# One transformer layer on one core: an opening in another order (rows ahead of weights, modulation in two column halves), and the first attention units prepared in twelve steps

## The chip, the cores and the metric

The kernel runs on one core of one Trainium2 chip. The metric is device time in microseconds (us) of one execution. All timed runs below are of the same program on the same inputs; the profile is one further execution that the hardware profiler recorded.

## What is computed

One layer of a hybrid diffusion backbone, over 2048 latent tokens of width 1024 and 256 context tokens, all in f32. Cut to what bears on this case:

```python
mod_x = silu(c) @ w_mod + b_mod          # w_mod (1024, 6*1024); six vectors of 1024
sh1, sc1, g1, sh2, sc2, g2 = split(mod_x, 6)
mod_c = silu(c_ctx) @ w_mod + b_mod
sh1c, sc1c = the first two of split(mod_c, 6)

h_c = rmsnorm(ctx, norm1_g) * (1 + sc1c) + sh1c
p_c = h_c @ w_in[:, :256]                # keys and values of the context only
h_x = rmsnorm(x, norm1_g) * (1 + sc1) + sh1
p_x = h_x @ w_in                         # k 128 | v 128 | q 512 | u 512 | vg 512 | gate 1024 | gate 1024
k, q = rmsnorm per head, rotary on latent tokens
attn = softmax(q @ [k_c; k_x].T) @ [v_c; v_x]      # 8 query heads, 2 key heads, head width 64
gm = gelu(u) * (gm_ws @ rmsnorm(gelu(vg)) + gm_bs) # in chunks of 128 tokens
x = x + g1 * ((sigmoid(ga) * (attn @ w_br_attn) + sigmoid(gb) * (gm @ w_br_gm)) @ w_out)
h2 = rmsnorm(x, norm2_g) * (1 + sc2) + sh2
x = x + g2 * (square(relu(h2 @ w_ff1)) @ w_ff2)
```

So nothing of a projection can begin before the vectors `sh1`, `sc1`, `sh1c` and `sc1c` are known: 1024 x 2048 of `w_mod` have to be read and multiplied with two conditions first.

## The kernel before, in words

The program is written out straight, with no loops on the chip, in four stages: `project()` (normalization, modulation, the input projection, keys, queries, the gated branch), `attend()` (32 units: four blocks of 512 queries, four pairs of heads in each, two of them to a key head), `merge()` and `ffn()`. `build()` (from L1464) calls them in turn.

A precise product is made of three matmuls: each operand is split into a rounded high part and a remainder, and `mm3` (L176) issues high x high, high x low and low x high; these are the lines L178, L179 and L180 in every view. `split` (L143) makes the two parts: the cast of the high part is L146 (ACT) or L148 (DVE), and the remainder is L150. `transposes` (L182, the matmul is L184) turns tiles on TensorE (PE) with an identity.

**The opening.** `mod_head` (L239) loads the two conditions, `norm1_g` and the first 2048 of `b_mod` in columns (one value of 4 bytes to a partition at a time, L244 to L253), on the queues of SP and ACT. It makes silu, a column per k (k counts eight slices of 128 channels) and condition, and multiplies for each k four halves of 512 columns of `w_mod` with a stationary operand two columns wide (L270): four banks, 32 matmuls. The rows of the result are copied (L276), turned by 16 small transposes, and `b_mod` is added (L285); L289 makes the scale `G1 = (1 + sc1) * norm1_g`, and `S1` holds the shift. Both are one tile of 8 k x 2 conditions. The rows of ctx are loaded at k = 2, those of x at k = 6, behind the weights of the k before them on SP's queue.

`h_build` (L434) is a generator with a step for each k: the rows of normalized x are turned on PE, ACT applies scale and shift (L443), DVE casts (L148) and subtracts (L150). `project()` (L706) takes all eight steps for the context, then all eight for block 0, and then the products of the keys and values: `token_mm` (L479) sums eight k for two tiles of 128 tokens into one bank, 256 columns each. The first two weight tiles of `w_in` (`w_tiles`, L451: four k of 256 columns each) serve these. After them come the wide products of 512 columns: queries, the two halves of the gated branch, and the gates.

**The gates and what lies among them.** For each block of 512 tokens, `project()` runs 16 gate steps (c = 0 to 3, two destinations, m = 0 and 1); `gate_mm` is 24 products of 512 columns. Behind each step of blocks 1 to 3 one step of `mod_rest` (L291) runs: the other four modulation vectors, summed on DVE one k a step, each with a load of 512 KB of `w_mod`. Behind the steps of the last block with c > 1, or c = 1 and the second destination, seven steps of `tail()` (L1470) run: it prepares units 0 and 1 of attention. A unit loads its queries from DRAM (`load`), ACT casts them (`cast`), DVE subtracts (`remainder`), and PE turns high parts and remainders, ACT copying the result (`queries`, the copy is L1567). `maxima` takes two banks, multiplies turned queries with keys (L1589), and DVE reduces each bank to its maxima (L1595 for the context, L1600 else); `reference` makes of them the offset of the softmax, and `low_queries` turns the remainders with it. `kb_build` (L757) makes copies of the keys with halves of partitions exchanged. When all gates are done `build()` runs out what is left of `tail()` and of `mod_rest`, and `attend()` begins with the scores of unit 0 (L1633).

**What sets the order.** A scheduler places the instructions of each engine as dependences and buffers allow. `order()` (L1504) adds rules after the program is written: new tiles of one tag (buffer class) are taken in program order; instructions in a range of `pins` keep program order on all engines, those in `fixed` on PE and DVE, those in `steady` on all but SP. Only `pins` around the loads of gm_ws and rope and around `mod_rest` lie in `project()`; `fixed` covers `attend()`. There are eight PSUM banks of 512 columns.

## Time and profile before

| what | value |
|---|---|
| time, median of 3 runs | 3026.22 us (3025.89 to 3028.58) |
| the profiled execution's own time | 3029.68 us |
| its span | 3027.9 us |
| PE busy | 2989.3 us, 99% |
| DVE busy | 2028.3 us, 67% |
| ACT busy | 1354.3 us, 45% |
| POOL (GpSimd) busy | 563.2 us, 19% |
| DMA, mean | 160 GB/s |
| mean granted clock of PE | 0.998 |
| span from 0 to 71 us: PE busy | 58.20 us |
| span from 71 to 711 us: PE busy | 640.00 us |
| span from 711 to 773 us: PE busy | 59.07 us |

The span is what the profiler saw between the first and the last instruction; the execution's own time is 1.8 us more. PE's busy time is the union of its matmuls, which overlap. It tells that PE worked on something, not at what width: a matmul with two columns of result rows and one with 128 count alike. In the views a row reads line, engine, operation, output and inputs by tile name without buffer numbers; a square bracket holds the idle time ahead of the row and who ended it. Tile names begin with the tag: `w` for weights, `t` for the working buffers, `m` for rows of x and ctx, `ts` for small vectors, `b` for PSUM banks.

### The profile page before, as it was taken

To read this page: it belongs to the slowest core of one execution; us is meant where nothing else is said; L and a number is where in the kernel's file an instruction comes from. 1 tells how busy PE (TensorE), PEld (TensorE's weight loads), DVE (VectorE), ACT (ScalarE), POOL (GpSimd) and SP (SyncE) were. 2 spreads that over 40 slices of the span, in tenths; PEclk is the share of its full clock that TensorE was granted. 3 is DMA by queue.
4 is the path that set the end of the run, shared out by engine and by line. 5 is a ranking of instruction groups with operands and counts; after the bars stand their busy time and mean duration, and the time that the engine had idled before them with its cause. 6 is when DMAs were issued, how large, how long until landed. Compare 5 with 4: busy or idle time off the path is not lost.

```text
span 3027.9 us, 39850 instructions
## 1 busy us (share of the span) xinstructions
PE 2989.3 (99%) x14980; PEld 2304.8 (76%) x14980; DVE 2028.3 (67%) x2984; ACT 1354.3 (45%) x2043; POOL 563.2 (19%) x419
## 2 busy tenths in 40 slices
PE   8999999999999999999999999999999999999999
PEld 4888888887665656655888878887878888888887
DVE  5837567586777778886655688776665666654455
ACT  4443434343555555554322254444553344444432
POOL 0000000000689999990000000000000000000000
PEclk9999999999999999999999999999999999999999
DMA  6354656645000000012755549889766544436665
GB/s 217 109 184 119 220 155 187 183 129 164 29 15 12 15 22 19 26 33 95 240 180 180 167 141 329 310 304 316 241 210 222 197 154 151 152 144 218 210 221 194
DMA packets 332179, 485.53 MB, mean 160 GB/s; under 512 B 33969, under 2 KB 166321, under 8 KB 331986
## 3 DMA queue, kind: packets, MB, share of 16 engines
q1 hardware_dynamic: 324002, 478.38, 47.9%
q10 hardware_dynamic: 7984, 4.61, 0.5%
q8 instruction: 117, 1.92, 0.3%
q14 instruction: 76, 0.62, 0.1%
HBM read 348.56 MB, written 134.35 MB: 159 GB/s over the span
## 4 chain that ended last, share of the span: by engine, by line
PE 93%; DVE 3%; DMA 2%; ACT 1%; issue 1%; SPq 1%; ACTq 0%; DVEq 0%
PE b L1244 13%; PE b L1245 13%; PE b L1243 13%; PE b L178 11%; PE b L180 11%; PE b L179 11%; PE b L1633 9%; PE b L1653 8%; PE b L1589 2%; PE b L184 2%; DVE ts L1600 1%; DMA ts<-in_b_mod 1%; PE b L1695 0%; DMA w<-in_w_in 0%; DMA f<-x_d 0%
## 5 line engine op out<-in xcount | busy, mean ns | idle before, releaser
L1349 DVE TENSOR_TENSOR f<-f,f 128x1024 fp32r<-128x1024 f32 x224 | 264.5, 1221 | 251.4 <-ACT f L1348 251.3
L1600 DVE TENSOR_REDUCE ts<-b 128x1 f32<-128x512 f32 x512 | 311.7, 682 | 98.4 <-PE b L1589 98.3
L1244 PE MATMUL b<-f,f 128*128 128x512 f32 x896 | 350.4, 391 | 4.8 <-DVE f L1349 4.7
L1348 ACT CAST f<-f 128x1024 fp32r<-128x1024 f32 x224 | 224.7, 1052 | 287.4 <-PE b L1244 275.1
L1243 PE MATMUL b<-f,f 128*128 128x512 f32 x896 | 350.2, 391 | 1.3 <-ACT f L1348 1.3
L1245 PE MATMUL b<-f,f 128*128 128x512 f32 x896 | 349.4, 390 | 0.0
L1633 PE MATMUL b<-t,t 64*128 64x512 f32 x2304 | 331.4, 400 | 0.8 <-DVE ts L1600 0.8
L1633 PEld LDWEIGHTS b<-t,t 64*128 64x128 f32 x2304 | 227.1, 184 | 70.0 <-issue 26.2
L1676 POOL TENSOR_TENSOR ac<-ac,p 128x512 f32<-128x512 f32 x204 | 267.6, 1346 | 45.1 <-ACT p L1643 45.1
L1676 POOL TENSOR_TENSOR ac<-ac,t 128x512 f32<-128x512 f32 x146 | 232.9, 1623 | 0.0
L1643 ACT ACTIVATE p<-b 128x512 f32<-128x512 f32 x384 | 206.8, 599 | 49.9 <-PE b L1633 41.4
L1244 PE MATMUL b<-hl,f 128*128 128x512 f32 x576 | 224.4, 390 | 1.8 <-DVE hl L1006 1.8
L1245 PE MATMUL b<-hl,f 128*128 128x512 f32 x576 | 224.2, 389 | 0.0
L1243 PE MATMUL b<-hl,f 128*128 128x512 f32 x576 | 224.1, 389 | 0.0
L150 DVE TENSOR_TENSOR w<-w,w 128x1024 fp32r<-128x1024 f32 x120 | 146.7, 1223 | 96.1 <-ACT w L146 73.0
L178 PE MATMUL b<-t,w 128*128 128x512 f32 x512 | 202.8, 396 | 0.1
L1244 PEld LDWEIGHTS b<-f,f 128*128 128x128 f32 x896 | 168.5, 188 | 43.0 <-DVE f L1349 8.4
L180 PE MATMUL b<-t,w 128*128 128x512 f32 x512 | 199.7, 390 | 0.0
L179 PE MATMUL b<-t,w 128*128 128x512 f32 x512 | 199.5, 390 | 0.0
L1243 PEld LDWEIGHTS b<-f,f 128*128 128x128 f32 x896 | 168.6, 188 | 37.1 <-ACT f L1348 2.4
L1245 PEld LDWEIGHTS b<-f,f 128*128 128x128 f32 x896 | 168.6, 188 | 34.8
L146 ACT CAST w<-w 128x1024 fp32r<-128x1024 f32 x120 | 126.0, 1050 | 152.5 <-DMA w<-in_w_in 115.0
(231 smaller groups left out, 6033.0 us busy)
## 6 DMA issues: line engine op xcount, KB each, us to landing
w<-in_w_in SPq DMA_DIRECT2D x120, 512.0 KB
ao_d<-f SPq DMA_DIRECT2D x224, 256.0 KB
f<-ao_d SPq DMA_DIRECT2D x112, 512.0 KB
f<-w2o_d SPq DMA_DIRECT2D x112, 512.0 KB
f<-in_w_ff SPq DMA_DIRECT2D x48, 1024.0 KB
w2o_d<-f SPq DMA_DIRECT2D x112, 256.0 KB
md<-in_w_mod SPq DMA_DIRECT2D x32, 512.0 KB
f<-x_d SPq DMA_DIRECT2D x64, 256.0 KB
```

The costliest lines, as they stand in the source:

```text
L178: mm(ps, sh, mh, start=start, stop=False)
L179: mm(ps, sh, ml, start=False, stop=False)
L180: mm(ps, sl, mh, start=False, stop=stop)
L1243: mm(ps, wh, hh, start=start and k == 0, stop=False, skip_group_check=True)
L1244: mm(ps, wh, hl, start=False, stop=False, skip_group_check=True)
L1245: mm(ps, wl, hh, start=False, stop=k == len(w) - 1, skip_group_check=True)
L1348: nc.scalar.copy(h, f32(l))
L1349: nc.vector.tensor_tensor(out=l, in0=f32(l), in1=f32(h), op=ALU.subtract)
L1600: nc.vector.tensor_reduce(out=self.mx[:, t, h, c : c + 1], in_=ps[h], axis=AX.X, op=ALU.max)
L1633: self.nc.tensor.matmul(ps[h], keys[h], q[rows[h]], start=n == 0, stop=n == len(steps) - 1, skip_group_check=True,)
L1653: nc.tensor.matmul(self.o[h * HD : (h + 1) * HD, :], k.V[c][:, i, self.kv * HD : (self.kv + 1) * HD], pt[h], start=j == 0, stop=j == NKT - 1,)
L1676: nc.gpsimd.tensor_tensor(out=self.acc[e][:, h], in0=old[:, h], in1=pt[h], op=ALU.add)
```

## The change

Six things, all in `mod_head`, `project` and `tail`:

1. Small vectors. `c`, `c_ctx`, `norm1_g` and `b_mod` are loaded as 8, 8, 8 and 16 rows of 128 (512 bytes each) on SP's queue, into one tile; one PE transpose turns it and DVE copies it out (`cols`, in the one buffer of tag `t1`).
2. Rows ahead of weights. The loads of ctx and x are issued before any of `w_mod`.
3. Modulation in two column halves. `mod_half` loads for each k the same 512 columns of shift and of scale as one transfer (pieces of 2 KB in place of rows of 4 KB). silu is padded with zeros to 64 columns (`wide`), and the products of the shift go to partitions 0 to 63 of one bank, those of the scale to 64 to 127. Half 0 serves k = 0 to 3 of h, half 1 serves k = 4 to 7; `S1` and `G1` are two tiles each. Each half is copied once by ACT and turned by four full transposes.
4. Keys and values k by k. `project()` builds one k of the context's and of block 0's h at a time; `token_step` issues the products of that k for all six token tiles at once, so three banks stay open over all k. Two k of half 1's modulation stand between the steps. All of it is in `fixed`, that is, in program order on PE and DVE.
5. `mod_rest` steps run also behind the gates with c > 1 of block 0 (eight more steps, so the sums end eight gates earlier).
6. `tail()` is written anew in twelve steps, one behind each gate step with c > 0 of the last block. Maxima come in threes (six banks); the load, cast and remainder of unit 1 lie between those of unit 0.

The diff, cut:

```diff
@@ -240,58 +241,74 @@
         nc, I = self.nc, self.I
         warm = self.small([1])
         nc.scalar.activation(warm, self.ones[:, :1], AF.Tanh)
...
+        rows = self.t2([P])
+        srcs = [
+            v.rearrange("(k p) -> k p", p=P)
+            for v in (I["c"][0], I["c_ctx"], I["norm1_g"][0], I["b_mod"][0, : 2 * D])
+        ]
+        lo = 0
+        for v in srcs:
+            n = v.shape[0]
+            nc.sync.dma_start(rows[lo : lo + n], v)
+            lo += n
+        self.xc = self.x_load(I["ctx"][0], CTX // P, self.m4)
+        wide = self.t2([KC, HD])
+        nc.gpsimd.memset(wide, 0.0)
+        pt = self.bank([lo])
+        nc.tensor.transpose(pt, rows[:lo], self.ident[:lo, :lo])
+        cols = self.sb("t1", [lo])
+        nc.vector.tensor_copy(cols, pt)
+        craw = cols[:, : 2 * KC].rearrange("p (j k) -> p k j", j=2)
+        gcol, bcol = cols[:, 2 * KC : 3 * KC], cols[:, 3 * KC :]
         th = self.small([KC, 2])
         nc.scalar.activation(th, craw, AF.Tanh, scale=0.5)
         nc.vector.tensor_scalar(
             out=th, in0=th, scalar1=0.5, scalar2=0.5, op0=ALU.mult, op1=ALU.add
         )
         nc.vector.tensor_tensor(out=self.silu, in0=th, in1=craw, op=ALU.mult)
...
+        nc.vector.tensor_copy(wide[:, :, :2], self.silu)
+        self.x0 = self.x_load(self.x_block(0), TT, self.t4)
+        self.h_scale(self.xc)
+        self.h_scale(self.x0, dve=True)
+        self.halves_1 = [self.mod_half(i, wide, bcol, gcol) for i in range(2)]
+        for _ in self.halves_1[0]:
+            pass
+        self.wq, self.wt = [], self.w_tiles()
+        self.w_first = next(self.wt) + next(self.wt)
+
+    def mod_half(self, half, wide, bcol, gcol):
+        nc = self.nc
+        H = KC // 2
+        src = self.I["w_mod"][0][:, : 2 * D].rearrange("(k p) (i c) -> k p i c", p=P, i=2)
+        ps = self.bank([TB])
         for k in range(KC):
...
+            w = self.w4([2, TB])
+            nc.sync.dma_start(w, src[k][:, :, half * TB : (half + 1) * TB])
             for i in range(2):
...
+                nc.tensor.matmul(
+                    ps[i * HD : (i + 1) * HD, :], wide[:, k, :], w[:, i, :],
+                    start=k == 0, stop=k == KC - 1,
+                )
+            if k % 2:
+                yield
+        row = self.t2([TB])
+        nc.scalar.copy(row, ps)
+        pt = self.bank([H, P])
+        self.transposes(
+            pt.rearrange("p j c -> p (j c)"), [row[:, j * P : (j + 1) * P] for j in range(H)]
+        )
+        for i, dst in enumerate((self.S1[half], self.G1[half])):
+            lo = i * KC + half * H
             nc.vector.tensor_tensor(
...
+                out=dst, in0=pt[:, :, i * HD : i * HD + 2],
+                in1=bcol[:, lo : lo + H].unsqueeze(2).broadcast_to([P, H, 2]), op=ALU.add,
             )
         nc.vector.scalar_tensor_tensor(
...
+            out=self.G1[half], in0=self.G1[half], scalar=1.0,
+            in1=gcol[:, half * H : (half + 1) * H].unsqueeze(2).broadcast_to([P, H, 2]),
             op0=ALU.add, op1=ALU.mult,
         )
...
+        yield
 
     def mod_rest(self):
         nc, I = self.nc, self.I
...
@@ -488,6 +504,14 @@
                     k == 0, k == KC - 1,
                 )
         return ps
+
+    def token_step(self, ps, h, w, k):
+        for t in range(2 * len(ps)):
+            self.mm3(
+                ps[t // 2][:, t % 2, :], h[k][0][:, t * P : (t + 1) * P],
+                h[k][1][:, t * P : (t + 1) * P], w[k][0], w[k][1],
+                k == 0 and t % 2 == 0, k == KC - 1, skip=True,
+            )
 
     def wide_mm(self, h):
         ps = [self.bank([2, 256]) for _ in range(TT)]
...
@@ -704,25 +728,48 @@
         return self.I["x"][0, b * TB : (b + 1) * TB]
 
     def project(self, tail, mod):
-        self.wq, self.wt = [], self.w_tiles()
         self.KA, self.V = [], []
-        wkv = self.w_next() + self.w_next()
-        xs = self.x0
+        begin, wkv = self.here(), self.w_first
         hc, h = [], []
-        for _ in self.h_build(self.xc, self.G1[:, :, 1], self.S1[:, :, 1], hc):
+        parts = ((self.h_build(self.xc, 1, hc), hc), (self.h_build(self.x0, 0, h), h))
+        done = [[self.bank([2, 256]) for _ in range(n)] for n in (CTX // P // 2, TT // 2)]
+        H = KC // 2
+        rest = self.halves_1[1]
+
+        def tiles():
+            for build, _ in parts:
+                next(build, None)
+
+        def products(k):
+            for (_, hs), ps in zip(parts, done):
+                self.token_step(ps, hs, wkv, k)
+
+        tiles()
+        for k in range(1, H):
+            tiles()
+            if k > 1:
+                products(k - 2)
+            next(rest)
+        products(H - 2)
+        next(rest)
+        products(H - 1)
+        for _ in rest:
             pass
+        for k in range(H, KC + 1):
+            tiles()
+            if k > H:
+                products(k - 1)
+        self.fixed.append(range(begin, self.here()))
         at = self.here()
         self.gm_load()
         self.rope_consts()
         self.pins.append(range(at, self.here()))
-        for _ in self.h_build(xs, self.G1[:, :, 0], self.S1[:, :, 0], h, lo=True):
-            pass
-        fin_c = self.kv_block(hc, CTX // P, None, wkv)
+        fin_c = self.kv_block(hc, CTX // P, None, wkv, done[0])
         self.gm_consts()
         for b in range(NB):
             if b:
                 wkv = self.w_next() + self.w_next()
-            fin = self.kv_block(h, TT, b, wkv)
+            fin = self.kv_block(h, TT, b, wkv, None if b else done[1])
             self.q_mm(h, b, self.rope_tables("q", b))
             if b == 0:
                 fin_c()
...
@@ -736,7 +783,7 @@
                     wg = self.w_next() + self.w_next()
                     for m in range(2):
                         self.gate_mm(h, b, c, wg, dst, m)
-                        if b:
+                        if b or c > 1:
                             at = self.here()
                             next(mod, None)
                             self.pins.append(range(at, self.here()))
...
@@ -1458,29 +1501,42 @@
         units = [Unit(self, n) for n in range(NU)]
 
         def tail():
-            u = units[0]
+            u, v = units[:2]
             u.load()
             u.cast()
-            yield from self.kb_build()
+            keys = self.kb_build()
+            for _ in range(NB + 1):
+                next(keys)
+            yield
+            for _ in keys:
+                pass
             u.remainder()
             yield
             u.queries()
-            while u.todo:
-                u.maxima(1)
-                yield
-                yield
-            units[1].load()
-            units[1].cast()
-            units[1].remainder()
+            yield
+            u.maxima(3)
+            v.load()
+            yield
+            u.maxima(3)
+            v.cast()
+            yield
+            u.maxima(3)
+            v.remainder()
+            yield
+            u.maxima(3)
+            yield
+            v.queries()
+            u.maxima(3)
+            yield
+            u.maxima(3)
             u.reference()
-            for _ in range(4):
-                yield
-            units[1].queries()
+            yield
+            v.maxima(3)
+            yield
+            v.maxima(3)
             yield
             u.low_queries()
-            for _ in range(6):
-                units[1].maxima(1)
-                yield
+            yield
 
         prep0, mod = tail(), self.mod_rest()
         self.project(prep0, mod)
```

How it moves the instructions. First PE in the opening. Before, all products of block 0 stand behind the last of its transposes (`t` are rows of x on the left of the first rows, bank b_659 the last k; b_670 is the bank of the context's keys and values):

```order
L184 MATMUL b_659<-ident,t_33_388 128x128
L184 MATMUL b_659<-ident,t_34_390 128x128
L184 MATMUL b_659<-ident,t_35_392 128x128
L184 MATMUL b_659<-ident,t_36_394 128x128
L178 MATMUL b_670<-w_470,t_66_498 128x256
L179 MATMUL b_670<-w_471,t_66_498 128x256
L180 MATMUL b_670<-w_470,t_67_499 128x256
L178 MATMUL b_670<-w_470,t_70_507 128x256
```

After, PE's order between two steps of products has this form (w_526 and w_530 are two k of `w_mod`'s second half, t_5_304 the padded silu, m and t_9 to t_12 the rows of ctx and x):

```order
L178 MATMUL b_438<-w_426,t_53_448 128x256
L179 MATMUL b_438<-w_427,t_53_448 128x256
L180 MATMUL b_438<-w_426,t_54_449 128x256
L288 MATMUL b_479<-w_526,t_5_304 64x512 x2
L288 MATMUL b_479<-w_530,t_5_304 64x512 x2
L184 MATMUL b_536<-ident,m_300 128x128
L184 MATMUL b_536<-ident,m_302 128x128
L184 MATMUL b_545<-ident,t_9_315 128x128
L184 MATMUL b_545<-ident,t_10_317 128x128
L184 MATMUL b_545<-ident,t_11_319 128x128
L184 MATMUL b_545<-ident,t_12_321 128x128
L178 MATMUL b_436<-w_426,t_57_459 128x256
```

In the new order a step of products is followed by two k of modulation and by the six transposes of the next k of h; before, these kinds of work stood apart.

DVE in the same place, before. S and G, 16 values each, stand behind the remainder of the first tile of `w_in` and ahead of all of h:

```order
L150 TENSOR_TENSOR w_471<-w_468,w_470 128x1024
L285 TENSOR_TENSOR S_75<-b_416,ts_300 128x16
L285 TENSOR_TENSOR G_74<-b_416,ts_300 128x16
L289 SCALAR_TENSOR_TENSOR G_74<-G_74,ts_296 128x16
L150 TENSOR_TENSOR w_477<-w_474,w_476 128x1024
L148 CAST t_66_498<-t_69_503 128x256
L150 TENSOR_TENSOR t_67_499<-t_69_503,t_66_498 128x256
```

After, the second pair of vectors (S_1, G_1) stands behind a k of h and behind the remainders of the first two tiles of the wide projection (w_905, w_911):

```order
L148 CAST t_82_543<-t_85_550 128x512
L150 TENSOR_TENSOR t_83_544<-t_85_550,t_82_543 128x512
L150 TENSOR_TENSOR w_905<-w_902,w_904 128x1024
L150 TENSOR_TENSOR w_911<-w_908,w_910 128x1024
L302 TENSOR_TENSOR S_1_77<-b_626,t_7_308 128x8
L302 TENSOR_TENSOR G_1_75<-b_626,t_7_308 128x8
L306 SCALAR_TENSOR_TENSOR G_1_75<-G_1_75,t_7_308 128x8
L148 CAST t_92_634<-t_95_639 128x256
```

So the vectors come in two pieces now, and DVE has to have those two tiles' data before it gets to the second.

PE at the handover, in the last block's gates, before (b_6417 is a gate's bank, t_1156 the turned queries):

```order
L180 MATMUL b_6417<-t_953_5293,w_6261 128x512
L184 MATMUL b_6458<-ident,t_1140_6391 128x128 x4
L184 MATMUL b_6465<-ident,t_1140_6391 128x128 x4
L1589 MATMUL b_6473<-t_199_1116,t_1156_6463 128x256
L1589 MATMUL b_6474<-t_1142_6396,t_1156_6463 128x256
```

After:

```order
L180 MATMUL b_6411<-t_964_5329,w_6282 128x512
L184 MATMUL b_6439<-ident,t_1134_6335 128x128 x4
L184 MATMUL b_6446<-ident,t_1134_6335 128x128 x4
L178 MATMUL b_6454<-t_896_4998,w_6177 128x512
L179 MATMUL b_6454<-t_897_4999,w_6177 128x512
L180 MATMUL b_6454<-t_896_4998,w_6178 128x512
```

24 products further on, where that gate ends:

```order
L179 MATMUL b_6454<-t_965_5330,w_6281 128x512
L180 MATMUL b_6454<-t_964_5329,w_6282 128x512
L1645 MATMUL b_6482<-t_199_1115,t_1157_6444 128x256
L1645 MATMUL b_6483<-t_1136_6340,t_1157_6444 128x256
L1645 MATMUL b_6482<-t_199_1115,t_1157_6444 128x256
L1645 MATMUL b_6483<-t_1136_6340,t_1157_6444 128x256
```

The turned queries were used by the very next matmuls; now a gate's 24 products stand between the transposes and the maxima, which are L1645 in the new file.

More of the change, by code (lines that the diff above doesn't have):

```diff
@@ L199, in constants @@
             nc.vector.memset(self.lead[h * HD : h * HD + 1], 1.0)
-        self.G1 = cp.tile([P, KC, 2], F32, name="G1")
-        self.S1 = cp.tile([P, KC, 2], F32, name="S1")
+        self.G1, self.S1 = (
+            [cp.tile([P, KC // 2, 2], F32, name=f"{n}1_{i}") for i in range(2)] for n in "GS"
+        )
         self.G2 = cp.tile([P, KC], F32, name="G2")
@@ L274, in mod_head @@
-        for n in range(4):
-            r = rows[n // 2][:2, (n % 2) * 512 : (n % 2 + 1) * 512]
-            nc.scalar.copy(r, ps[n][:2])
-        pt = self.bank([2 * KC, 2])
-        for j in range(2 * KC):
-            nc.tensor.transpose(
-                pt[:, j, :], rows[j // KC][:2, (j % KC) * P : (j % KC + 1) * P],
-                self.ident[:2, :2],
-            )
-        for i, dst in enumerate((self.S1, self.G1)):
-            sl = slice(i * KC, (i + 1) * KC)
+        nc.vector.tensor_copy(wide[:, :, :2], self.silu)
@@ L526, in kv_block @@
         for t0 in range(0, nt, 2):
-            ps = self.token_mm(h, w, t0)
+            ps = done[t0 // 2] if done else self.token_mm(h, w, t0)
             nc.vector.tensor_copy(
```

60 lines of the change are left out of this document (14 added, 46 removed).

## Prediction

> **What bounds the kernel now.** I read the waits of TensorE (PE) first, up to the point where attention begins. The columns are the waiting line, what it waited for, the total in us, how often and the longest.
>
> ```profile
> PE b L270 <- DVE silu L258: 6.9, 1, 6.9
> PE b L270 <- DMA w<-in_w_mod: 3.8, 2, 2.0
> PE b L1589 <- ACT t L1567: 2.0, 1, 2.0
> PE b L178 <- ACT t L443: 1.0, 1, 1.0
> ```
>
> Beyond these PE hardly waits in 720 us: from the first wide projection to attention it is the bound, and nothing off it counts. Only two places can give time back: the opening, where PE is idle or does work of little width, and the handover at 711 us. The timeline of PE shows where the opening ends: the last products of block 0's keys and values (256 columns), and the first wide product (512 columns).
>
> ```profile
> 70.77 0.28 PE L179 MATMUL b<-w,t 128*128 128x256 f32 x1
> 70.89 0.28 PE L180 MATMUL b<-w,t 128*128 128x256 f32 x1
> 71.01 0.40 PE L178 MATMUL b<-w,t 128*128 128x512 f32 x1
> ```
>
> So the opening lasts 71.0 us, and one 256-column product costs the step between rows, 0.12 us. What made it late is in the chain of work (start, length, what the path waited in):
>
> ```profile
> 2.21 16.45 DMA ts<-in_b_mod
> ...
> 21.16 8.58 DMA t<-in_x
> 29.80 10.50 DMA w<-in_w_in
> ```
>
> The load of `b_mod` into columns holds SP's queue until 18.67 (the transfer that follows waits for its lane), the rows of x come behind most of the weights, and the first `w_in` tile lands at 40.3. After that come 30.7 us of modulation vectors, h and products. Rates of transfer, in windows of 3 us (last two columns: share of the engines, GB/s; before them the granted clock):
>
> ```profile
> 24.00:27.00 3.00, 3.00 (x5) 0.39 (x4) 0.00 (x0) 0.00 (x0) 0.00 (x0) 0.51 1.02 371
> ...
> 42.00:45.00 3.00, 2.88 (x28) 2.54 (x29) 1.27 (x5) 2.34 (x5) 0.00 (x0) 1.00 1.03 356
> ```
>
> The first is x and `w_mod` in rows of 4 KB, the second mostly `w_in` in pieces of 1 and 2 KB.
>
> **The modulation products.** In PE's timeline before (each matmul of this f32 kind leaves two records, 32 make the 64):
>
> ```profile
> 22.73 10.44 PE L270 MATMUL b<-w,silu 128*2 128x512 f32 x20 [2.04 <-DMA w<-in_w_mod]
> ...
> 34.91 7.03 PE L270 MATMUL b<-w,silu 128*2 128x512 f32 x16 [1.74 <-DMA w<-in_w_mod]
> ```
>
> Eight matmuls in 7.03 us: 0.88 each, 28 us for all. The change pads the two conditions to 64 columns and sends shift and scale to the two halves of the output partitions. That form runs already, in attention's values:
>
> ```profile
> 788.06 3.65 PE L1653 MATMUL b<-p,t 128*64 128x512 f32 x16
> 791.55 1.89 PE L1653 MATMUL b<-t,t 128*64 128x512 f32 x8
> 793.37 0.87 PE L184 MATMUL b<-ident,t 128*128 128x128 f32 x6
> ```
>
> 24 records, twelve matmuls, in 5.31 us: 0.44 each, since the two halves overlap. I take 0.44, so a k of both (shift, scale) costs 0.88 instead of 1.76. The bounds for it are 0.88 and 1.76.
>
> **The opening, walked through.** Durations of ScalarE (ACT) and VectorE (DVE), grouped by shape (total, then mean ns):
>
> ```profile
> L146 ACT CAST w<-w 128x1024 fp32r<-128x1024 f32 x6 | 6.4, 1061 | 8.8 <-DMA w<-in_w_in 5.6 <-DVE t L150 3.2
> L443 ACT ACTIVATE t<-b,S,G 128x512 f32<-128x512 f32 x8 | 5.8, 804 | 0.0
> L443 ACT ACTIVATE t<-b,S,G 128x256 f32<-128x256 f32 x8 | 3.9, 576 | 0.7 <-DVE G L289 0.7
> L276 ACT COPY t<-b 2x512 f32<-2x512 f32 x4 | 2.0, 570 | 0.0
> ```
>
> ```profile
> L150 DVE TENSOR_TENSOR t<-t,t 128x512 fp32r<-128x512 f32 x7 | 4.9, 694 | 0.2
> L150 DVE TENSOR_TENSOR w<-w,w 128x1024 fp32r<-128x1024 f32 x3 | 3.7, 1219 | 0.0
> L148 DVE CAST t<-t 128x512 fp32r<-128x512 f32 x7 | 2.9, 421 | 0.0
> L150 DVE TENSOR_TENSOR t<-t,t 128x256 fp32r<-128x256 f32 x4 | 1.7, 426 | 0.1
> L148 DVE CAST t<-t 128x256 fp32r<-128x256 f32 x4 | 1.1, 286 | 0.0
> ```
>
> One k of h costs DVE 0.71 for the context and 1.12 for block 0; a weight split costs it 1.22.
>
> 1. Transfers. The four small row loads go ahead and I let the stream of large ones begin at 4 us (chosen: four issues, then the first bytes). Six tiles of context and x, 0.524 MB each at 385 GB/s (chosen; 371 in the row), 1.36 us each: to 12.2. Eight `w_mod` tiles in 2 KB pieces at 360: 1.46 each, to 23.8; with 0.8 for landing (chosen) the last is there at 24.6. Scaling of the rows and the turned vectors are hidden under these loads; without that cover they would cost their few us. Two `w_in` tiles in 1 KB pieces at 300 (chosen) land by 28.1, the second half of `w_mod` from 29.6 to 39.8, two tiles of the first wide projection at about 43 and 45.
> 2. First half: last k 0.88 (25.5), copy 0.57, four turns 0.5, three small DVE operations 0.6: S and G for k 0 to 3 at 27.6.
> 3. Then cast and split of the second `w_in` tile (28.1 + 1.06 + 1.22 = 30.4) and one k of h (1.83): first operands complete at about 32.3.
> 4. From there PE runs in a fixed order. Each of the four products steps has six blocks of three: 18 x 0.12 = 2.16. Between them lie the second half's matmuls, 2 x 0.88 and about 0.2 for changing widths, and six turns (0.77). From 32.7, when k 0 and 1 of the second half and the next turns are done: 2.16 + 1.96 + 0.77 + 2.16 + 1.96 + 2.16 + 1.96 = 13.1, so the last matmul of the second half ends at 45.9. Here PE itself is late, no longer the transfers (39.8).
> 5. Copy 0.6, the fourth products 2.16 and the turns 0.5 on PE, then the vectors: S and G for k 4 to 7 at 49.5. On DVE the two splits of the wide projection's tiles stand ahead of these vectors; their data land at 45, cast and split end at about 48.9, so they just don't decide. If the stream is slower they do.
> 6. DVE: four k of h (4 x 1.83) and two more splits (2 x 1.22), 9.8 us, with 1.2 of waits behind ACT's casts: the last h at about 61. Products for it 2.16, eight turns for the spatial weights 1.0: the wide projection starts at 64.5.
>
> That is 71.0 - 64.5 = **6.5 us** less. With 400 GB/s and shorter steps it would be 62.5, with 300 GB/s 68.4: between 8.5 and 2.5.
>
> At one place a rule bears on this. In the timeline above PE waited 2.04 us at 22.73; the records that followed were 0.85 us apart instead of 0.43 until about 27, and the clock in the window 24 to 27 is 0.51: some 2 us lost. My walk's longest gap is 1.2 us (28.4 to 29.6), so I charge nothing; were it to reach two, the row says 2 us, 3017.7. The Trainium skill, TensorE: Matmul & The Clock Gate, section HAM oscillation, puts the limit at gaps of more than about 3.4 us, by which even then nothing would be lost: 3015.7. The trace's gap of 2.04 that did cost clock speaks for the shorter limit.
>
> **The handover.** PE before, from the last gate ahead of it to the first scores:
>
> ```profile
> 710.98 0.39 PE L180 MATMUL b<-t,w 128*128 128x512 f32 x1
> 711.21 1.03 PE L184 MATMUL b<-ident,t 128*128 128x128 f32 x8
> 714.22 0.81 PE L1589 MATMUL b<-t,t 64*128 64x256 f32 x8 [1.97 <-ACT t L1567]
> ...
> 743.72 1.09 PE L1589 MATMUL b<-t,t 64*128 64x512 f32 x2 [0.32 <-DVE ts L1600]
> ...
> 759.52 1.10 PE L1589 MATMUL b<-t,t 64*128 64x512 f32 x2 [0.31 <-DVE ts L1595]
> ...
> 772.55 1.20 PE L1633 MATMUL b<-t,t 64*128 64x512 f32 x8
> ```
>
> Turned queries are used at once (1.97 of idling, 2.2 with what lies round it), and twice a pair of maxima waits for DVE: 0.32 + 0.31 idle, and 1.09 for two where eight scores take 1.20, so 0.8 too much each. Sum 2.2 + 0.6 + 1.6 = 4.4. In the change a gate of 24 matmuls (5.5 us at the 0.23 between the first two rows) stands between the turned queries and their use, maxima come six banks at a time, which eight banks hold, and the modulation's sums have left DVE there. Six reductions and a split fit a gate's time. New is that unit 0's turned maxima are used at once by the first scores; six of the eight matmuls ahead of it need them not, so I charge 0.4 (between 0 and 2.0, the wait of the same kind above). **4.0 us** less; bounds 2.4 and 4.4.
>
> **Other edits, at nothing.** Eight modulation steps move into block 0's last gates: VectorE work and 0.5 MB loads beside a PE that does not wait there; without that cover each costs a sum per gate. The rope load waits for the one `t1` buffer (until 49.5) and the fourth wide tile queues behind it on SP; it is needed 16 us after 64.5. ACT's loads of norm vectors come after its last h; VectorE needs them after 61. From the first scores on the orders are the same.
>
> Sum: 6.5 + 4.0 = 10.5. The profiled execution took 3029.68 us (span 3027.9), 3.46 over the median 3026.22; I apply the difference to the median: **3015.7**. Its own range is 3012 to 3020.
>
> **The rivals.**
> - The handover gives nothing: a new wait (the turned maxima, or ACT's casts ahead of a gate's tanh) takes the place of the old ones. For it: the old waits came of just such neighbours. Against: a gate lies between now. Then 6.5 alone: 3019.7.
> - The column halves do not overlap here, as transfers deal them out k by k. Each k costs 1.76: the first half ends 3 us later, PE's part in step 4 grows by 6 x 0.88 = 5.3; start at 72.8, 1.8 later than before, less 4.0 of the handover: 3024.0, no change. Against: the values' rows.
> - Slower: PE stays at half clock through the whole stop-and-go opening, as in the window with 0.51. Then a k costs 1.76, products 4.32, six turns 1.5; the first half ends at 28.5, step 4 at 63.7, the second vectors at 69.3, and the four last products at half rate bring the start to 93: 22 later, less 4.0, 3044. It decides from 16.5 us of lost PE time on (6.5 + 4.0 + 6). Against: in that window full work brought the clock back in 4 us, and step 4 is full work. The Trainium skill's page named above has it as a rule: a wait that passes its window starts the next burst cold.
> - It doesn't do what it says, with VectorE's two splits deciding the second vectors: a part of the range, 68.4, 3019.6.
>
> **How the numbers follow.** The forecast, with its slower streams, 0.62; no gain in the handover 0.14; no overlap 0.12; half clock 0.06; mixtures of these 0.06, mostly still faster. 0.2% is 6 us, about what a measurement of this kernel can tell from no change. Faster 0.81, same 0.13, slower 0.06. The range 3010 to 3023 leaves out the two cases without overlap and at half clock, 0.18 together, and little else.
>
> **What would show it.** First wide product near 64.5; second-half matmuls spaced 0.44; second vectors on DVE near 49.5; no `b_mod` in the chain; PE's waits between 700 and 770 without the 2.0. Wrong if the first h comes after 36, if PEclk shows 0.5 after 30, or if the first scores are less than 6 us earlier.

## The result, and the profile after

The changed kernel takes **3012.22 us** (median of 4 runs, 3011.96 to 3013.43), the kernel before in the same session 3026.91: a ratio of 0.995, 95% interval 0.9938 to 0.9962. That is 14.7 us less; the forecast was 10.5 less, 3015.7 us with a range of 3010 to 3023. Run again later beside the experiments it took 3014.36 against 3028.28, a ratio of 0.9955 (0.9941 to 0.9968). Such intervals are 7 to 8 us wide. So the finer steps below go by the stages of the profiles, which repeat far better.

First the windows by stage. They are cut at the first wide product and the first scores. The columns are the stretch, its length, then busy time and records of PE, of its weight loads, VectorE (DVE), ScalarE (ACT) and POOL; then PE's clock, the DMA share and GB/s. Before:

```profile
0.00:71.01 71.01, 58.21 (x281) 30.30 (x282) 34.13 (x105) 30.02 (x49) 0.83 (x7) 0.98 0.68 222
71.01:772.55 701.54, 698.61 (x3386) 581.79 (x3384) 458.35 (x903) 287.29 (x401) 26.98 (x32) 1.00 0.52 159
```

After:

```profile
0.00:59.85 59.85, 43.89 (x273) 29.33 (x274) 30.67 (x88) 28.84 (x44) 1.31 (x8) 1.00 0.79 271
59.85:757.84 697.99, 697.26 (x3387) 581.36 (x3385) 462.40 (x925) 286.93 (x404) 26.66 (x32) 1.00 0.52 159
```

The opening gave 71.01 - 59.85 = 11.16 us (forecast 6.5), the handover 701.54 - 697.99 = 3.55 (forecast 4.0): 14.7 together, all of the timed gain. What follows the first scores is the same program, and differs by 2.6 us in these two executions (3027.9 - 772.55 and 3010.6 - 757.84); over all the profiles below it moves by up to 4.4 us, which is the noise of one execution.

The first row holds the surprise. PE is idle for 71.01 - 58.21 = 12.8 us of the opening before and for 59.85 - 43.89 = 16.0 after: it waits more, not less. What fell is its work, by 14.3 us. PE's own rows show it, grouped by shape, before and after:

```profile
L270 PE MATMUL b<-w,silu 128*2 128x512 f32 x64 | 31.3, 647 | 10.7 <-DVE silu L258 6.9 <-DMA w<-in_w_mod 3.8
```

```profile
L288 PE MATMUL b<-w,t 128*64 128x512 f32 x64 | 18.1, 697 | 11.5 <-DMA w<-in_w_mod 11.5
```

The same 32 matmuls keep PE busy for 18.1 us in place of 31.3 (1.7 of the 31.3 are the stretch at half clock behind the wait at 22.73, windows of 21 to 24 at 0.92 and 24 to 27 at 0.51). In PE's timeline of the changed kernel:

```profile
14.08 9.09 PE L288 MATMUL b<-w,t 128*64 128x512 f32 x28 [10.33 <-DMA w<-in_w_mod]
...
27.81 1.08 PE L288 MATMUL b<-w,t 128*64 128x512 f32 x4 [0.63 <-DMA w<-in_w_mod]
...
33.13 1.94 PE L288 MATMUL b<-w,t 128*64 128x512 f32 x8
...
59.85 0.48 PE L178 MATMUL b<-w,t 128*128 128x512 f32 x1
```

Eight records in 1.94 us are four matmuls, 0.47 to 0.49 each: the halves overlap. The first 14.08 us hold nearly all of the idling, and from 30.2 on PE hardly stops. At the handover PE's timeline has no wait any more between the turned queries and the first maxima; two waits of 0.31 for VectorE stand among the later ones:

```profile
696.26 1.03 PE L184 MATMUL b<-ident,t 128*128 128x128 f32 x8
...
702.68 0.97 PE L1645 MATMUL b<-t,t 64*128 64x256 f32 x10
...
744.19 0.50 PE L178 MATMUL b<-t,w 128*128 128x512 f32 x1 [0.31 <-DVE ts L1651]
...
751.13 0.50 PE L1645 MATMUL b<-t,t 64*128 64x512 f32 x1 [0.31 <-DVE ts L1656]
...
757.84 1.30 PE L1689 MATMUL b<-t,t 64*128 64x512 f32 x8
```

### The profile page after: what moved, and what is told of

Its sections match the earlier page's. It is cut to its first block, busy times and chain, and to the rows that moved or that the text cites. A ratio compares the mean times of both kernels' runs of the same rounds, so it can differ in the third digit from the quotient of the medians.

```text
span 3010.6 us, 39824 instructions
## 1 busy us (share of the span) xinstructions
PE 2971.5 (99%) x14973; PEld 2300.4 (76%) x14973; DVE 2024.5 (67%) x2989; ACT 1353.1 (45%) x2041; POOL 564.9 (19%) x420
## 4 chain that ended last, share of the span: by engine, by line
PE 95%; DVE 2%; DMA 2%; ACT 1%; issue 1%; SPq 0%; DVEq 0%; ACTq 0%
PE b L1287 13%; PE b L1288 13%; PE b L1286 13%; PE b L178 11%; PE b L180 11%; PE b L179 11%; PE b L1689 9%; PE b L1709 8%; PE b L1645 2%; PE b L184 2%; DMA w<-in_w_mod 1%; PE b L1751 0%; PE b L288 0%; DMA f<-x_d 0%; DVE ts L1656 0%
## 5 line engine op out<-in xcount | busy, mean ns | idle before, releaser
L1287 PEld LDWEIGHTS b<-f,f 128*128 128x128 f32 x896 | 168.5, 188 | 44.1 <-DVE f L1392 9.5
```

What stands on the lines that cost most here:

```text
L1287: mm(ps, wh, hl, start=False, stop=False, skip_group_check=True)
```

## The experiments

The theory after the result: from the first vectors on, PE's own work sets the opening (about 33 us of it lie between 24.5 and 59.85), and ahead of them the arrival of rows and first half. Rivals: VectorE's chain from vectors to h, or the order of the loads alone. All twelve runs, with three numbers of each profile: the start of the first modulation matmul, the first wide product, and the length from there to the first scores. The medians come from four sessions, in which the kernel before took 3026.91 to 3028.28 us, so compare the ratios.

| run | median us | ratio to before (95%) | first modulation matmul | first wide product | to the first scores |
|---|---|---|---|---|---|
| before (profile) | | | 6.85 | 71.0 | 701.5 |
| changed (profile) | 3012.22 | 0.9950 (0.9938-0.9962) | 14.08 | 59.9 | 698.0 |
| changed again | 3014.36 | 0.9955 (0.9941-0.9968) | 13.93 | 59.7 | 698.0 |
| opening alone | 3015.55 | 0.9959 (0.9946-0.9971) | 14.54 | 60.3 | 703.1 |
| tail and sums alone | 3024.56 | 0.9989 (0.9980-0.9998) | 6.93 | 72.1 | 697.9 |
| changed, sums late | 3013.61 | 0.9951 (0.9939-0.9964) | 14.10 | 59.9 | 698.5 |
| vectors on the same rows | 3024.34 | 0.9989 (0.9981-0.9998) | 14.58 | 71.5 | 698.0 |
| rows behind | 3025.15 | 0.9993 (0.9984-1.0002) | 6.14 | 71.7 | 698.0 |
| rows behind, PE busy | 3024.36 | 0.9985 (0.9977-0.9994) | 6.16 | 68.6 | 698.0 |
| small vectors in columns | 3018.13 | 0.9968 (0.9956-0.9981) | 15.28 | 64.7 | 698.0 |
| splits behind | 3012.78 | 0.9952 (0.9940-0.9965) | 13.79 | 59.5 | 698.0 |
| products behind | 3016.90 | 0.9960 (0.9946-0.9974) | 14.66 | 60.8 | 698.0 |
| quarters | 3010.39 | 0.9942 (0.9930-0.9955) | 14.01 | 57.6 | 698.0 |
| quarters, splits behind | 3011.05 | 0.9943 (0.9930-0.9955) | 14.79 | 58.3 | 698.0 |

Four of the profiles have the same opening (changed, changed again, opening alone, sums late). Their wide products start at 59.7 to 60.3, and the whole of this spread lies ahead of the first modulation matmul, which starts when its weights have come: from there it takes 45.77 to 45.80 us in all four. So where the order of the loads is that of the changed kernel, the experiments below are compared from the first modulation matmul on. The opening of before varies too: 71.0 here, 72.1 where it stands with the new tail.

**The two parts.** The opening alone keeps `tail()` and the place of `mod_rest` as they were; its edit to the changed kernel (the tail alone is the same edit the other way round, on the kernel before):

```diff
-                        if b or c > 1:
+                        if b:
...
-                        if b + 1 == NB and c:
-                            next(tail, None)
+                            if b + 1 == NB:
+                                for _ in range(7):
+                                    next(tail, None)
...
-            u, v = units[:2]
+            u = units[0]
```

> The new opening alone, with the tail and the modulation steps as before. If the two parts of the change add, this takes the opening's part of the gain, 11.2 us (first wide product at 59.85 as in the changed kernel, 71.01 before): 3015.7 us. Rival: the early start only moves waits, and the handover grows by what the opening gave: over 3018.

> The new tail and the modulation steps of block 0 alone, on the opening as before. If the parts add: 3.5 us less than before, 3023.4 us, with 698.0 us between the first wide product and the first scores (701.5 before). Rival: it needs the early opening to have its loads in time, and gives under 1 us: 3026.

Each part gives its own stage what it gives in the whole: the opening alone starts its wide products at 60.3, the tail alone takes 697.9 to the scores. But the opening alone needs 1.6 us more from its first wide product to the scores than the kernel before. Its timeline shows the wait of before, and what came behind it:

```profile
703.60 0.90 PE L1634 MATMUL b<-t,t 64*128 64x256 f32 x8 [1.97 <-ACT t L1612]
...
705.44 0.63 PE L180 MATMUL b<-t,w 128*128 128x512 f32 x1
705.87 0.63 PE L178 MATMUL b<-t,w 128*128 128x512 f32 x1
...
708.29 0.39 PE L179 MATMUL b<-t,w 128*128 128x512 f32 x1
```

A gate's products step by 0.43 us in place of 0.23 for some three us. The windows, of this run and of before at the same point, show PE's clock:

```profile
703.00:706.00 3.00, 2.40 (x12) 1.89 (x13) 2.84 (x4) 1.03 (x3) 0.00 (x0) 0.70 0.81 247
706.00:709.00 3.00, 3.00 (x12) 2.34 (x11) 1.92 (x3) 0.69 (x1) 0.00 (x0) 0.73 0.78 267
```

```profile
714.00:717.00 3.00, 2.79 (x17) 2.28 (x18) 3.00 (x5) 0.64 (x2) 0.00 (x0) 1.00 0.94 316
```

The same gap of 1.97 us cost the clock in one execution (0.70 and 0.73) and not in the other (1.00). So the wait that the new tail removes was worth 2 us in the profile of before, and 3.5 where the clock fell.

**The sums of modulation, late again.** One line: `if b or c > 1:` is `if b:` again.

> The changed kernel without the eight modulation steps in block 0, so that the sums of the other four vectors end eight gates later, among the tail's steps. If the new order of the tail carries the handover's gain and the sums cost VectorE nothing that PE waits for: as the changed kernel, 3012.2 us. Rival: the sums beside the maxima are what PE waited for: 1.0 to 2.0 us more, 3013.2 to 3014.2.

0.55 us in its stage (698.54 against 697.99), between the two; the times can't tell it. PE's timeline has the sum's two matmuls back among the maxima, and three pairs of maxima after them take 1.38 in place of 0.96:

```profile
727.29 1.88 PE L341 MATMUL b<-md,ones 128*128 128x512 f32 x4
729.00 1.04 PE L184 MATMUL b<-ident,t 128*128 128x128 f32 x8
729.97 1.38 PE L1645 MATMUL b<-t,t 64*128 64x512 f32 x6
```

That leaves some 3 of the 3.55 us to the new order of the tail.

**The halves on the same rows.** The two conditions stand in the middle of the padded silu, and two windows of it put shift and scale on the same 32 partitions of one sum:

```diff
-                    ps[i * HD : (i + 1) * HD, :], wide[:, k, :], w[:, i, :],
-                    start=k == 0, stop=k == KC - 1,
+                    ps[:32, :], wide[:, k, a : a + 32], w[:, i, :],
+                    start=k == 0 and i == 0, stop=k == KC - 1 and i == 1,
```

with `a = 31 - 30 * i`.

> Shift and scale are summed on the same 32 output partitions, one after the other, in place of two halves that overlap; transfers, copies and turns as in the changed kernel. Theory (PE's own work sets the opening from the first vectors on): a k costs 1.76 us in place of 0.97, the first half ends 3.6 later, since the transfers come every 1.3, and the second half adds 8 x 0.79 = 6.3: 9.9 more, 3022.1 us, first wide product at 69.8. Rival (VectorE's splits of h set it, PE's additional work is hidden): only the first half's 3.6 and little more, 3016.

```profile
14.58 16.25 PE L289 MATMUL b<-w,t 128*32 128x512 f32 x32 [10.82 <-DMA w<-in_w_mod]
...
33.32 3.62 PE L289 MATMUL b<-w,t 128*32 128x512 f32 x8
...
71.53 0.47 PE L178 MATMUL b<-w,t 128*128 128x512 f32 x1
```

Four matmuls take 3.62 in place of 1.94, and the opening is 11.7 us longer (11.2 from the first modulation matmul on): all that it had gained. VectorE hides none of it, so the rival falls. It is 1.7 more than expected: 0.5 because the first modulation matmul came later in this execution, and most of the rest because the first half takes 16.25 us and not 16 x 0.905 = 14.5, as its first matmuls ran at half speed. The records of that product in the changed kernel, up to 18 us (duration in ns: least, median, most), show the same; after 18 us their median is 592:

```profile
L288 PE MATMUL b<-w,t x10: 1057/1061/1116, 14.1 to 17.6; 128*64 128x512 f32 x10
```

PE starts at half speed for 3.5 us (the clock's column says 1.00 there). In the changed kernel that lies under transfers that come every 1.35 us; where PE is the slower one it costs.

**Rows behind the first half.** The loads of ctx and x move behind the loads of half 0; nothing else changes:

```diff
         self.halves_1 = [self.mod_half(i, wide, bcol, gcol) for i in range(2)]
+        for _ in range(4):
+            next(self.halves_1[0])
+        self.xc = self.x_load(I["ctx"][0], CTX // P, self.m4)
+        self.x0 = self.x_load(self.x_block(0), TT, self.t4)
+        self.h_scale(self.xc)
+        self.h_scale(self.x0, dve=True)
         for _ in self.halves_1[0]:
             pass
```

> The loads of ctx and x stand behind the first half of the modulation weights, and all else is as in the changed kernel. Theory: the bytes ahead of the first h are the same, but the normalization, which in the changed kernel lies beside the weights' loads (last row tile scaled at 21.4, vectors at 26.3), now comes behind the last row: landed 24.6, square 1.1, chain 3.0, four scalings 2.7, so 31.4 in place of 25.9 for the first turns: 5.5 more, 3017.7 us. Rival: the order of the loads does not matter, as their sum is the same: 3012.2.

The opening is 11.85 longer, twice the forecast. The windows show why it is not the normalization alone:

```profile
18.00:21.00 3.00, 0.00 (x0) 0.00 (x0) 1.49 (x9) 2.71 (x5) 0.00 (x0) 0.84 1.02 408
...
33.00:36.00 3.00, 2.81 (x12) 1.68 (x13) 2.93 (x6) 2.01 (x3) 0.00 (x0) 0.50 0.82 266
36.00:39.00 3.00, 3.00 (x17) 1.51 (x14) 1.84 (x5) 0.59 (x2) 0.00 (x0) 0.81 1.02 318
```

PE stopped at 16.57, its clock halved 3.5 us later and came back at about 37 (worked out from the 0.84 and the 0.81 of these windows). To size that, the next run gives PE matmuls that nobody needs in the gap (`busy` issues so many into a bank of their own):

```diff
+        if half == 0:
+            busy(11, w[:, 0, :])
         row = self.t2([TB])
...
+        if half == 0:
+            busy(4, row)
```

> The rows behind the first half of the modulation weights as in the run before, and PE is given 15 matmuls without use (11 while it waits for the copied row, 4 while it waits for the rows of x), so that its clock should stay up where it fell to 0.50 from 20 to 37 us; they write a bank that nobody reads. Theory (most of the 11.9 us is the normalization that lies open, the clock the smaller part): first wide product at 69 to 70, 2 to 3 us less than without, 3022. Rival (the clock is most of it): 65.4, that is the 5.5 us of the open normalization alone, 3017.7.

The clock stayed at 1.00 throughout, and the wide products start at 68.6, 3.1 us earlier. But the work in the gap earned only 1.7 of that, as the last matmuls of the second half show, with it and without:

```profile
48.19 1.94 PE L290 MATMUL b<-w,t 128*64 128x512 f32 x8
```

```profile
49.91 1.94 PE L290 MATMUL b<-w,t 128*64 128x512 f32 x8
```

The other 1.4 came later. With rows behind, the clock fell a second time, after a wait of 1.48 us at 62.36 (its rows stand further below); with PE busy a wait of 1.68 us at 60.83 was followed by windows at 1.00. So the matmuls without use have not been shown to prevent the second fall. Of the other 8.8, 6.0 are the open normalization (first product of h at 36.85 in place of 30.81). In the rest PE waits for VectorE, VectorE for ACT, and ACT, as far as can be read, for a wide tile (the profile names no releaser for its 2.96 us):

```profile
60.83 0.38 PE L178 MATMUL b<-w,t 128*128 128x256 f32 x1 [1.68 <-DVE t L148]
```

```profile
53.48 1.69 ACT L474 ACTIVATE t<-b,S,G 128x256 f32<-128x256 f32 x3 [1.77 <-DVE G L319]
58.13 1.05 ACT L146 CAST w<-w 128x1024 fp32r<-128x1024 f32 x1 [2.96 <-issue]
59.08 1.90 ACT L474 ACTIVATE t<-b,S,G 128x512 f32<-128x512 f32 x3
```

In this run SP's queue holds the load of that tile behind the rope load, issued at 53.41 when the second vectors free its buffer; in the changed kernel that load goes ahead of the rope. This chain is read from the trace and was not tried by itself.

**Small vectors in columns**, as before the change, on the new order:

```diff
-            nc.sync.dma_start(rows[lo : lo + n], v)
...
+        nc.scalar.dma_start(
+            bcol, I["b_mod"][:, : 2 * D].rearrange("o (k p) -> p (o k)", p=P)
+        )
```

> The small vectors loaded in columns as before (c on SP's queue, the others on ACT's), and all else as in the changed kernel. Theory: the load of b_mod in columns takes until 18.7 and a large transfer behind it on SP's queue waits for its lane, so that some six tiles come after it: half 0 some 4 us later, 3016.5 us. Rival: on rows it is hidden, since b_mod is needed at 25.9 only: 3012.2. Upper end, were all rows held: 3021.

4.8 us, where the theory had some 4: the first half's last matmul ends 4.25 later (28.78 for 24.53). The chain of work names the load again, and the tile that waited for it:

```profile
2.20 16.19 DMA ts<-in_b_mod
18.41 3.81 DMA w<-in_w_mod
22.26 3.51 PE b L281 x7
```

**VectorE's chain.** Three of the remainders of the wide tiles are made to follow the last h.

```diff
+            if idx > self.h_end and i.engine == self.nc.vector.engine and late and count < 4:
+                count += 1
+                if count > 1:
+                    self.tc.add_manual_dep(i, self.h_last.name, dep, reason="order")
```

> Three of the remainders of the wide projection's weights, which VectorE does in the opening ahead of the second vectors and among the last four k of h, stand behind the last h there (3 x 1.22 = 3.7 us). Theory (PE's own work sets the end): PE idles only 0.2 us from 30.2 to 59.9, so at most 0.8 us less, 3011.6. Rival (VectorE's chain sets it): the second vectors come 0.5 to 1.7 earlier and the last h 2.4 on top: 3009.

The wide products start 0.3 us earlier (59.54), but so does the first modulation matmul: from there it takes 45.75 us in place of 45.77. The splits behind gained nothing. The products of k 0 to 3 behind the second vectors try the same from the other side:

```diff
-            if k > 1:
-                products(k - 2)
             next(rest)
...
         for k in range(H, KC + 1):
             tiles()
-            if k > H:
-                products(k - 1)
+            products(k - H)
+        for k in range(H + 1, KC):
+            products(k)
```

> The products of k 0 to 3 stand behind the second half's vectors in place of between its matmuls. Theory (PE's own work): the second half is then paced by its transfers (last landed about 39), PE idles some 3 to 5 us among them, and all 8 x 2.2 us of products come after: 2.6 us more, 3014.8. Rival (VectorE's chain): second vectors at 41.5 in place of 47.2, last h and end 5.7 earlier: 3006.5.

VectorE gets its second vectors at 40.37, over six us early, and finishes h early (its last subtraction starts at 52.20; at 56.63 in the changed kernel), and yet the wide products start 1.0 us later, at 60.83; 0.4 later, counted from the first modulation matmul (46.17 us in place of 45.77). PE did less while it waited for the half's tiles, and did it all afterwards:

```profile
40.37 0.17 DVE L302 TENSOR_TENSOR S<-b,t 128x8 f32<-128x8 f32 x1 [3.64 <-PE b L184]
...
52.20 0.69 DVE L150 TENSOR_TENSOR t<-t,t 128x512 fp32r<-128x512 f32 x1
```

VectorE's chain is not the bound. The cost is 0.4 and not 2.6: where 3 to 5 us of idling were expected, PE idles 1.0 more in this stretch than in the changed kernel (3.15 us against 2.18), and is busy for 0.6 less.

**Quarters: the theory's own forecast.** If PE's work is the bound, less of it must be faster. Even and odd k go to quarters of their own, 32 partitions each, and VectorE adds them with two more small sums a half:

```diff
-                    ps[i * HD : (i + 1) * HD, :], wide[:, k, :], w[:, i, :],
-                    start=k == 0, stop=k == KC - 1,
+                    ps[q : q + 32, :], wide[:, k, :32], w[:, i, :],
+                    start=k < 2, stop=k >= KC - 2,
```

with `q = i * HD + k % 2 * 32`.

> Modulation on four quarters of the output partitions, 32 each: shift and scale, even and odd k; two more small sums on VectorE for each half. Theory (PE's own work sets the opening, and four quarters overlap as two halves do): two k of the second half take 1.0 us in place of 1.9, its last matmul ends 3.9 earlier, at 40 where its transfers end too, second vectors at 43.7 in place of 47.2, first wide product at 56.5: 3008.9 us. Rivals: quarters overlap no further than halves, 3012.2; VectorE's chain holds the end, under 1 us less.

> The changed kernel once more, beside the three that follow: 3012.2 us, first wide product at 59.9, first scores at 757.8.

```profile
37.01 1.07 PE L289 MATMUL b<-w,t 128*32 128x512 f32 x8
...
57.56 0.48 PE L178 MATMUL b<-w,t 128*128 128x512 f32 x1
```

Four matmuls take 1.07 us in place of 1.94, and the wide products start 2.2 us earlier than in the changed kernel beside it. It is 2.2 and not 3.4: three of the second half's four pairs of k are that much shorter (2.6 us), the first still waits for its tiles, and the two more sums take a little of it back. In time it is 3010.39 against 3014.36; the two intervals overlap, so the stage speaks and not the time. It is the fastest kernel of this study.

> The quarters, and the remainders of the second to fourth tile of the wide projection behind the last h on VectorE. Theory (from the second vectors on PE's products, turns and waits take 12.5 us, and VectorE's 7.4 us for four k lie under them): as with the quarters alone, 56.5 and 3008.9. Rival (with PE relieved VectorE's chain is next): 1 to 2 us less than with the quarters alone, 3007.5.

58.3, no gain: this execution was 0.8 late from its first modulation matmul on, against quarters alone:

```profile
14.79 5.01 PE L289 MATMUL b<-w,t 128*32 128x512 f32 x16 [10.99 <-DMA w<-in_w_mod]
```

```profile
14.01 6.38 PE L289 MATMUL b<-w,t 128*32 128x512 f32 x20 [10.14 <-DMA w<-in_w_mod]
```

From there to the wide products it takes 43.50 us with the splits behind and 43.55 without. With PE relieved VectorE's chain is not next either.

## Why the prediction was right, and by which steps

Direction, range and both mechanisms held. The sum missed by 4.2 us: +4.65 in the opening, -0.45 at the handover. The walk, step by step:

| | forecast | measured |
|---|---|---|
| last matmul of the first half ends | 25.5 | 24.5 |
| first vectors | 27.6 | 26.4 |
| first products | 32.3 | 30.8 |
| last matmul of the second half ends | 45.9 | 44.1 |
| second vectors | 49.5 | 47.4 |
| last h | 61 | 57.3 |
| first wide product | 64.5 | 59.85 |

- **Transfers (steps 1 and 2).** 1 us early: the stream ran at 388 to 408 GB/s in the windows from 6 to 21 us where 385 and 360 were chosen. Pieces of 2 KB went hardly slower (385 to 391) than rows of 4 KB (396 to 408). The cold start of PE was not in the walk, and the transfers hid it.
- **PE between the halves (steps 3 to 5).** Sized right: 13.3 us from the first products to the last matmul, forecast 13.6, and the steps before and behind it 0.3 shorter each than forecast. PE was late there and not the transfers, as step 4 had it.
- **The end (step 6)** is the term that was off: 12.5 us from the second vectors to the wide products, forecast 15. The walk put VectorE's 9.8 us plus 1.2 of waits in a row, and then products and eight turns. These terms add up to 63.7 and not to the 64.5 of the walk, so 0.8 of the 2.5 us came in without a term. In the trace VectorE takes 10.0 us, PE works beside it with one stop of 0.21, four of the eight turns slip in between, and only 2.5 us are left. It treated VectorE as the bound of the last 12 us; the runs with other orders on VectorE showed that PE was. That the walk came within 2.5 us there is partly luck: PE's own work and waits happen to be about as long (12.5 us) as the row of VectorE's work with PE's remainder behind it.
- **Handover.** Forecast were 4.4 less a charge of 0.4 for a new wait. Idle time fell by 2.2 (2.93 to 0.73), nearly all of it the wait of 1.97, and PE's busy time by 1.35, of which 0.9 shows in the rows of the maxima (8.0 to 7.1 us for the same 40 records). Two terms were wrong and offset each other in part, which is luck: the 0.6 of waits for VectorE was counted as gained and stayed (0.31 and 0.31, before 0.32 and 0.31), and the wait that the 0.4 was charged for, in front of the first scores, did not come.
- **Edits at nothing.** The rope load and the wide tile behind it did cost nothing here, but with rows behind and PE busy the same queue held the tile that ACT seems to have waited for. The cover was real, and thin. Block 0's modulation steps are worth 0.55.
- **The rivals.** Without the overlap of halves the forecast was 3024.0; made so, the kernel took 3024.34. The agreement is closer than the working: the wide products started at 71.5 and not 72.8, and the kernel before took 3028.15 beside it, so it was 3.8 us faster and not 2.2. Half clock came to nothing here, since no gap after 25.3 us is longer than 0.7. VectorE's splits ahead of the second vectors cost nothing that shows (45.75 against 45.77).

The price of the clock's rule was weighed at 2 us for a gap of 2 us. More rows bear on it now. Besides the 2.04 of the prediction, waits of PE of 2.51 us (small vectors in columns; windows at 0.68 and 0.75 behind it), 3.21 (tail and sums alone; 0.93 and 0.51) and 10.5 were followed by a fall of the clock. Waits of 1.68 (PE busy) and 1.74 (before, at 34.91) were not. At two lengths both came: 1.97 as shown above, and 1.48, followed by full clock with the tail alone (at 22.92; windows at 1.00) and with rows behind by two windows at 0.74 and 0.69:

```profile
62.36 0.39 PE L178 MATMUL b<-w,t 128*128 128x256 f32 x1 [1.48 <-DVE t L148]
```

```profile
63.00:66.00 3.00, 2.91 (x18) 2.91 (x19) 2.93 (x7) 1.09 (x3) 0.00 (x0) 0.74 0.62 180
66.00:69.00 3.00, 3.00 (x21) 3.00 (x20) 1.65 (x4) 0.71 (x1) 0.00 (x0) 0.69 0.48 93
```

The Trainium skill, TensorE: Matmul & The Clock Gate, section What's actually happening, has the clock decided in windows of 3413 ns that run free of the program. The 3.5 us after the start of the 10.5 us gap and the two outcomes each of 1.48 and 1.97 agree with that. The limit of some 3.4 us for a gap, from its section HAM oscillation, does not: 1.48, 1.97, 2.04 and 2.51 us sufficed. Each of the falls behind waits of 1.48 to 3.21 us took 1.7 us of clock, summed over its two windows (3 x 0.30 + 3 x 0.27 for the 1.97), so the price of 2 us was a little high.

**What stays open.** How the gain of 11.16 divides among the edits has no single answer: without the overlap the opening is 11.7 us longer, with rows behind 11.85, with columns 4.8, without the interleaving 1.0. Counted from the first modulation matmul, the first and the last of these are 11.2 and 0.4. Each was undone alone, and the sum is far over the gain, for they lie in one chain. With rows behind or columns PE idles 22.9 and 20.5 us in place of 16.0; without the overlap it idles less (15.1) and works more. Rows ahead and turned vectors pay by keeping the waits down, the halves by the work. How long a gap must be to cost the clock was not tried by itself.

## What to carry to other kernels

Before costing the waits of a stage, subtract: length minus busy time. Where an engine is busy nearly all the time, its work decides, and a narrow matmul that keeps it "busy" at a 64th of its width is the first place to look. Put data that needs long preparation ahead of data that is used at once, and treat a wait of PE of 1.5 us or more as a wait plus a possible 1.7 us of lost clock behind it. When two executions differ in a stage, look for the first row at which they differ: here the start of the first modulation matmul explained the differences of 0.3 and 0.8 us in the runs with splits behind.

## What was not expected of the hardware

- Small f32 matmuls on separate quarters of the output partitions overlap for the most part: 0.905 us each alone (3.62 for four), 1.94 for four as halves, 1.07 as quarters, so 1.9 and 3.4 times. The Trainium skill, TensorE: Matmul & The Clock Gate, section Measured speedup vs the span model, has 2.38 for three column tiles, which lies between the two.
- PE's first 3.5 us of work ran at half speed, 1061 ns a record in place of 592, while the clock's column read 1.00.
